# A delta rule's last norm traced in one piece, fewer filling steps around it and in the second attention, and another form of a recurrence's sigmoid

## Chip, cores and metric

One core of one Trainium2 chip runs the whole program in one launch. The metric is the device time of that launch in microseconds. The kernel before took 1979.86 us, the median of 3 runs (1976.52 to 1980.83).

## The reference, cut to what matters

The reference is two small transformer stacks in a row on a sequence of 256 positions and 1024 channels, all in float32. The first stack has two layers; each is a feed-forward block, a mixer, and a feed-forward block. The mixer sums three gated branches: a latent attention (mla), a gated delta rule (gdn) and a second attention (moba; with 256 positions and blocks of 256 it is plain causal attention). The second stack has an even and an odd layer; the odd mixer joins a gated linear recurrence with a dilated attention.

```python
# gated delta rule, chunks of 64 positions, one after the other
v_new = u_i - w_i @ state
o_i   = q_i @ state + qk_i @ v_new
state = state * exp(gl_i) + k_i.T @ v_new
...
o = rms_norm(o, out_norm) * silu(z)          # o over 128 values of one head

# linear recurrence of the odd mixer
r = sigmoid(xc @ w_a + b_a)
i = sigmoid(xc @ w_x + b_x)
log_a = -8.0 * r * softplus(-lam)
a  = exp(log_a)
bt = sqrt(-expm1(2.0 * log_a)) * (i * xc)
h_t = a_t * h_(t-1) + bt_t
```

## The kernel before, in words

**Matrix products.** Every large product is made in three passes: operand and weight are each split into a rounded high part and the remainder, a low part. `chunk` (L254) loads a chunk of weights into a staging tile `st` on SyncE's queue (3 buffers) and splits it in pieces of up to 1024 columns: ScalarE writes the high part `whi` (L281), VectorE the low part `wlo` (L282), with 3 buffers each. `mm3` (L287) issues the three matmuls of one contraction block (L290, L291, L292); the third reads the low part of the weights where weights are the stationary operand.

**Filling.** Small, latency-bound work (attention heads, the delta rule) is a Python generator that yields where it would wait; large projections are generators too, which yield after each 12 matmuls. `_mix` (L187) steps the first and pulls from the second at a fixed ratio per yield, `_weave` (L201) alternates. A pull that begins a projection also calls `chunk` for its weights, and the pull after its last step evacuates it.

**Order.** The scheduler of the framework orders each engine's instructions by program order and a simulated timeline; an instruction that is ready in the simulation may go ahead of an earlier one that is not. From the inversion to the scan of the delta rule, TensorE alone is under `manual_schedule`: it keeps the order of tracing exactly, while VectorE, ScalarE and GpSimd do not. `issue_after(ins)` adds an edge, so that what is traced in the block on the engine of `ins` is queued behind `ins`.

**The mixer** (L679 and following). The second attention is mixed with the generator `keys` (L718) at 2.05: what is left of the earlier filling, then the preparation of the delta rule's keys woven with the first merge and half of a gate projection. Its heads go in four pairs; `attend_o` makes six transposes of the scores (pPT), copies them to PT (L625, ScalarE) and multiplies them with the values (pOT). Then the generator `rest` (L741), 32 steps, fills `gdn_invert` (0.65, woven with `gdn_rest`), `gdn_solve` (1.65) and `gdn_scan` (1.5): half a gate projection (8 steps), a merge (8), and the two halves of the last gate projection (16, four per chunk of weights). The last merge, which follows, reads the scan's result in its high and low parts `brh` and `brl`.

**`gdn_scan`** goes through four chunks c = 0 to 3. In each, TensorE adds two products in `po` (L1261, L1282); between them VectorE makes `gvn` (L1264) and the generator yields; ScalarE copies `po` to `on` (L1284, written `gon` in the profile), and it yields again. `norm(t, on)` squares on ScalarE, then reduces, takes a reciprocal square root (`rsqrt`, L313: twelve operations on four columns) and multiplies (L1242) on VectorE. `finish(t, on)` makes four transposes (pon), multiplies with the gate and splits into `brh` and `brl`.

**`lru_core`** (L1641) makes the recurrence's coefficients in two passes of 512 columns: VectorE takes the pre-activation out of PSUM negated (L1665), bounds it (L1668), ScalarE takes the exponential (L1669), VectorE adds 1 (L1671) and takes the reciprocal (L1672); ScalarE makes `la` and `lm`, later a square root. It fills the odd mixer's projections; the dilated attention (`dil_attn`) that follows has scores `dpr`, transposes pdPT, and as filling the product with the recurrence's result `yh`, `yl`.

Of the kernel before, what the change touches and what calls it, by code (L numbers as in the profile page):

```python
# [1 line left out]

# [1 line left out]

# [5 lines left out]
F32 = mybir.dt.float32  # L10
F32R = mybir.dt.float32r
I32 = mybir.dt.int32
AF = mybir.ActivationFunctionType
# [207 lines left out]
class _Net:  # L221
    def __init__(self, ctx, tc, w, x, params, consts, lru, out, pat, cat, np_, nc_):
        self.tc, self.nc, self.w, self.x_in, self.out = tc, tc.nc, w, x, out
        self.params, self.consts, self.lru = params, consts, lru
        self.pat, self.cat, self.n_params, self.n_consts = pat, cat, np_, nc_
        P = lambda name, bufs, **kw: ctx.enter_context(tc.tile_pool(name=name, bufs=bufs, **kw))
        ps = bass.MemoryType.PSUM
        self.keep = P("keep", 1)
        self.wst = P("wst", 3)
        self.whl = P("whl", 3)  # L230
        self.nrm = P("nrm", 1)
        self.acc = P("acc", 4, space=ps)
        self.misc = P("misc", 4, space=ps)
        self.tiny = P("tiny", 4)
        self.early = {}
        self.P = self.keep.tile([128, self.n_params], F32, name="P")
        self.C = self.keep.tile([128, self.cat["dil0"]], F32, name="C")

# [15 lines left out]
    def chunk(self, name, i, between=None):  # L254


        nc = self.nc
        if (name, i) in self.early:
            return self.early.pop((name, i))
        chunks = [(kt, sum(b - a for a, b in cols)) for cols, (_, kt) in STREAMS[name]]  # L260
        sizes = [128 * kt * cols for kt, cols in chunks]
        layer, j = divmod(i, len(chunks))
        off = layer * sum(sizes) + sum(sizes[:j])
        kt, cols = chunks[j]
        n = kt * cols
        st = self.wst.tile([128, WMAX], F32, tag="st", name="st")
        src = lambda a, m: bass.AP(tensor=self.w[name].tensor, offset=off + a, ap=[[n, 128], [1, m]])
        if between is None:
            nc.sync.dma_start(out=st[:, :n], in_=src(0, n))
        pieces = []  # L270
        step = WPIECE // cols
        for k0 in range(0, kt, step):
            kk = min(step, kt - k0)
            m = kk * cols
            if between is not None:
                between(k0)
                nc.sync.dma_start(out=st[:, k0 * cols:k0 * cols + m], in_=src(k0 * cols, m))
            s = st[:, k0 * cols:k0 * cols + m]
            hi = self.whl.tile([128, WPIECE], F32R, tag="whi", name="whi")
            lo = self.whl.tile([128, WPIECE], F32R, tag="wlo", name="wlo")  # L280
            self.hi = nc.scalar.activation(hi[:, :m], s, AF.Copy).ins  # L281
            nc.vector.tensor_tensor(lo[:, :m], s, hi[:, :m].bitcast(F32), op=OP.subtract)  # L282
            v = lambda t: t[:, :m].rearrange("p (k c) -> p k c", k=kk)
            pieces.append((k0, kk, v(hi), v(lo)))
        return pieces
# [393 lines left out]
    def mixer(self, l, gain):  # L679
        pool = lambda ctx, name, bufs, **kw: ctx.enter_context(  # L680
            self.tc.tile_pool(name=name, bufs=bufs, reuse_waits="tile", **kw))
        with ExitStack() as ctx:
# [5 lines left out]
            with ExitStack() as c2:  # L688
# [37 lines left out]

                got["gate2"] = []
                f2 = keys()
                brs[2] = _mix(self.heads(big, at, *self.moba_heads(at, *z), sc, nsc), f2, 2.05)
                _all(f2)  # L730
            with ExitStack() as c2:
                gp = pool(c2, "mxg", 1)
# [488 lines left out]
    def gdn_scan(self, big, wk, scal, out, us, sz, vq):  # L1221
# [12 lines left out]
        def norm(t, on):  # L1234

            junk = W("gj")
            nc.scalar.activation(junk, on, AF.Square)
            ss = self.tiny.tile([128, 4], F32, tag="sso", name="sso")
            nc.vector.reduce_sum(ss, h4(junk), axis=AX)
            nc.vector.scalar_tensor_tensor(ss, ss, 1.0 / 128, vq[:, 4 * t:4 * t + 4], op0=OP.mult, op1=OP.add)  # L1240
            r = self.rsqrt(ss, 4, "ro")
            nc.vector.tensor_tensor(h4(on), h4(on), bch(r), op=OP.mult)  # L1242
            return on

        def finish(t, on):
            p4 = h4(self.transposes("pon", lambda h: on[:, h * 128:(h + 1) * 128]))
# [6 lines left out]
        for c in range(4):  # L1253
# [26 lines left out]
            for h in range(4):  # L1280
                cc = slice(h * 128, (h + 1) * 128)
                mm(po[orow, cc], qkT[t][wr, h * 64:h * 64 + 64], vn[wr, cc],  # L1282
                   start=(c == 0 and h == 0), stop=True, skip_group_check=True)
            nc.scalar.activation(on[orow, :], po[orow, :], AF.Copy)  # L1284
            yield
            if c == 1:
                ons = [norm(0, on)]
            if c == 2:
                yield
                finish(0, ons[0])  # L1290
        r = norm(1, on)
        for _ in range(4):
            yield
        finish(1, r)
        yield
        return oh, ol

    def gdn_z(self, l, big, wk):
# [342 lines left out]
    def lru_core(self, big, wk, xc, wa, wx, hs):  # L1641
# [4 lines left out]
        nl = big.tile([128, 4], F32, name="nl")  # L1646
        nc.vector.tensor_scalar(nl, self.par("lru_lam", 4), -1.0, None, op0=OP.mult)
        self.softplus(sp, nl, 4)
        nc.vector.tensor_scalar(sp, sp, -8.0, None, op0=OP.mult)
        nb = big.tile([128, 8], F32, name="nb")  # L1650
        nc.vector.tensor_scalar(nb[:, 0:4], self.par("lru_ba", 4), -1.0, None, op0=OP.mult)
        nc.vector.tensor_scalar(nb[:, 4:8], self.par("lru_bx", 4), 0.5, None, op0=OP.mult)
        a, bt, m2 = B("la"), B("lb"), B("lm")
        yield
        for c in range(2):
            pr, pi = self.ps("plr"), self.ps("pli")
            for b in range(2):
                m = 2 * c + b
                nc.tensor.matmul(pr[:, b * S:(b + 1) * S], wa[:, m, :], xc[:, m, :], start=True, stop=True)
                nc.tensor.matmul(pi[:, b * S:(b + 1) * S], wx[:, m, :], xc[:, m, :], start=True, stop=True)  # L1660
            v = slice(2 * c, 2 * c + 2)
            r = wk.tile([128, 2, S], F32, tag="lr", name="lr")
            for b in range(2):
                m = 2 * c + b
                nc.vector.tensor_scalar(r[:, b, :], pr[:, b * S:(b + 1) * S], -1.0, nb[:, m:m + 1], op0=OP.mult, op1=OP.add)  # L1665
                nc.scalar.activation(bt[:, m, :], pi[:, b * S:(b + 1) * S], AF.Tanh, scale=0.5, bias=nb[:, 4 + m:5 + m])
            yield
            nc.vector.tensor_scalar(r, r, 80.0, None, op0=OP.min)  # L1668
            nc.scalar.activation(r, r, AF.Exp)  # L1669
            yield  # L1670
            nc.vector.tensor_scalar(r, r, 1.0, None, op0=OP.add)  # L1671
            nc.vector.reciprocal(r, r)  # L1672
            for b in range(2):
                m = 2 * c + b
                nc.scalar.activation(a[:, m, :], r[:, b, :], AF.Exp, scale=sp[:, m:m + 1])
                nc.scalar.activation(m2[:, m, :], r[:, b, :], AF.Tanh, scale=sp[:, m:m + 1])
            yield
            sq = wk.tile([128, 2, S], F32, tag="lsq", name="lsq")
            nc.gpsimd.tensor_tensor(sq, a[:, v, :], a[:, v, :], op=OP.mult)
            nc.vector.tensor_scalar(sq, sq, 1.0, -1.0, op0=OP.add, op1=OP.mult)  # L1680
            nc.gpsimd.tensor_tensor(m2[:, v, :], m2[:, v, :], sq, op=OP.mult)
            nc.vector.scalar_tensor_tensor(bt[:, v, :], bt[:, v, :], 1.0, xc[:, v, :], op0=OP.add, op1=OP.mult)
            yield
# [73 lines left out]
```

## Time and profile before

| | |
|---|---|
| median of 3 runs | 1979.86 us (1976.52 to 1980.83) |
| the profiled execution's own time | 1975.25 us |
| its span from first to last instruction | 1973.4 us |
| TensorE busy | 98% |
| VectorE busy | 78% |
| ScalarE busy | 55% |
| GpSimd busy | 6% |
| mean granted TensorE clock | 0.997 |

PE is TensorE's matmuls, PEld its weight loads, DVE is VectorE, ACT ScalarE, POOL GpSimd, SP SyncE. Times in rows are microseconds from the start of the span unless marked as ns. Where a tile is named `out<-in`, the instruction reads `in` and writes `out`; `L282` is line 282 of the kernel before. In a timeline the bracket at a row's end is the idle time before it and what released it.

### The profile page before, as it was taken

Reading aid. Unit: us, or ns where it says so; the run is one execution under the profiler, and the core shown is the slowest. Engines: PE = TensorE matmul, PEld = TensorE weight load, DVE = VectorE, ACT = ScalarE, POOL = GpSimd, SP = SyncE. Lnnn points to the kernel's source line nnn. Section 1 sums busy time; section 2 is a strip of 40 time slices with the busy share of each in tenths; the row PEclk is TensorE's granted clock in tenths of the full one; section 3 lists DMA queues with packets and bytes.
Section 4 is the critical chain, followed back from the end, with each engine's and each line's share of the span. In section 5 each row is a group of like instructions: output and inputs, shape, how many; then the busy total and the mean of one; then the engine's idle time right before and its main releaser. Section 6 shows DMA issues by size and latency. Waiting matters only on the chain.

```text
span 1973.4 us, 35062 instructions
## 1 busy us (share of the span) xinstructions
PE 1937.5 (98%) x14060; PEld 1772.7 (90%) x14060; DVE 1530.1 (78%) x2797; ACT 1091.0 (55%) x1766; POOL 122.8 (6%) x154
## 2 busy tenths in 40 slices
PE   7999999999999999999999999999999999989999
PEld 7889989899988988899898998889999989979998
DVE  6876889757787677769996678766978876978875
ACT  5555666534555555556664455554656654666653
POOL 0000130210000000001211100000000000210000
PEclk9999999999999999999999999999999999989999
DMA  6555544324555555554432345555245556426554
GB/s 243 190 184 191 178 154 145 108 87 143 181 190 182 202 176 190 187 183 182 150 129 87 108 171 184 187 188 188 90 167 180 186 178 215 147 76 213 177 179 137
DMA packets 50691, 327.18 MB, mean 166 GB/s; under 512 B 6624, under 2 KB 8672, under 8 KB 18528
## 3 DMA queue, kind: packets, MB, share of 16 engines
q1 hardware_dynamic: 49296, 324.09, 46.7%
q8 instruction: 110, 1.80, 0.4%
q10 hardware_dynamic: 1232, 0.85, 0.2%
q14 instruction: 53, 0.43, 0.1%
HBM read 323.87 MB, written 1.05 MB: 165 GB/s over the span
## 4 chain that ended last, share of the span: by engine, by line
PE 94%; DVE 4%; issue 1%; ACT 1%; DMA 0%; SPq 0%; DVEq 0%; ACTq 0%
PE pu L416 11%; PE pr L416 9%; PE pg L416 7%; PE pu L418 6%; PE pr L418 5%; PE pg L418 4%; PE pg L292 3%; PE pg L291 3%; PE pg L290 3%; PE pr L291 3%; PE pr L290 3%; PE pr L292 3%; PE pga L290 3%; PE pga L291 2%; PE pga L292 2%; PE pb L291 1%
## 5 line engine op out<-in xcount | busy, mean ns | idle before, releaser
L281 ACT ACTIVATE whi<-st 128x1024 fp32r<-128x1024 f32 (+2 forms) x628 | 650.7, 1037 | 696.0 <-PE pr L416 121.9
L282 DVE TENSOR_TENSOR wlo<-st,whi 128x1024 fp32r<-128x1024 f32 (+2 forms) x628 | 760.2, 1211 | 311.7 <-ACT whi L281 306.3
L416 PE MATMUL pu<-xx,whi 128*128 128x512 f32 x960 | 336.8, 395 | 0.0
L416 PE MATMUL pr<-gx,whi 128*128 128x512 f32 x792 | 272.3, 395 | 0.0
L418 PE MATMUL pu<-xx,wlo 128*128 128x256 f32 x960 | 264.1, 279 | 0.0
L416 PE MATMUL pg<-xx,whi 128*128 128x512 f32 x640 | 223.6, 394 | 0.0
L416 PEld LDWEIGHTS pu<-xx,whi 128*128 128x128 f32 x960 | 178.8, 188 | 39.3
L418 PE MATMUL pr<-gx,wlo 128*128 128x256 f32 x792 | 211.0, 279 | 0.0
L418 PEld LDWEIGHTS pu<-xx,wlo 128*128 128x128 f32 x960 | 180.8, 188 | 1.6
L418 PE MATMUL pg<-xx,wlo 128*128 128x256 f32 x640 | 175.7, 278 | 0.0
L416 PEld LDWEIGHTS pr<-gx,whi 128*128 128x128 f32 x792 | 144.4, 188 | 29.6
L418 PEld LDWEIGHTS pr<-gx,wlo 128*128 128x128 f32 x792 | 149.2, 188 | 5.4
L416 PEld LDWEIGHTS pg<-xx,whi 128*128 128x128 f32 x640 | 119.2, 188 | 26.7
L290 PE MATMUL pg<-xx,whi 128*128 128x256 f32 x448 | 128.0, 286 | 9.6 <-ACT whi L281 9.6
L292 PE MATMUL pg<-xx,wlo 128*128 128x256 f32 x448 | 127.9, 285 | 0.5 <-DVE wlo L282 0.5
L291 PE MATMUL pg<-xx,whi 128*128 128x256 f32 x448 | 127.6, 285 | 0.0
L418 PEld LDWEIGHTS pg<-xx,wlo 128*128 128x128 f32 x640 | 120.2, 188 | 1.1
L290 PE MATMUL pga<-xx,whi 128*128 128x256 f32 x384 | 112.2, 292 | 0.0
L291 PE MATMUL pga<-xx,whi 128*128 128x256 f32 x384 | 108.7, 283 | 0.0
L292 PE MATMUL pga<-xx,wlo 128*128 128x256 f32 x384 | 108.7, 283 | 0.0
L290 PEld LDWEIGHTS pg<-xx,whi 128*128 128x128 f32 x448 | 86.6, 193 | 10.6 <-ACT whi L281 9.6
L292 PEld LDWEIGHTS pg<-xx,wlo 128*128 128x128 f32 x448 | 86.5, 193 | 1.0 <-DVE wlo L282 0.8
(565 smaller groups left out, 4451.0 us busy)
## 6 DMA issues: line engine op xcount, KB each, us to landing
st<-in_w_in_dram SPq DMA_DIRECT2D x52, 1024.0 KB, 4.8
st<-in_ffb_w_in_dram SPq DMA_DIRECT2D x44, 1024.0 KB, 4.7
st<-in_ffa_w_in_dram SPq DMA_DIRECT2D x43, 1024.0 KB, 4.8
st<-in_ffn_w_gate_dram SPq DMA_DIRECT2D x22, 1024.0 KB, 4.8
st<-in_ffn_w_up_dram SPq DMA_DIRECT2D x22, 1024.0 KB, 4.7
st<-in_ffa_w_out_dram SPq DMA_DIRECT2D x16, 896.0 KB, 4.5
st<-in_ffb_w_out_dram SPq DMA_DIRECT2D x16, 896.0 KB, 4.5
st<-in_ffn_w_down_dram SPq DMA_DIRECT2D x16, 896.0 KB, 4.6
```

The costliest lines, as they stand in the source:

```text
L281: self.hi = nc.scalar.activation(hi[:, :m], s, AF.Copy).ins
L282: nc.vector.tensor_tensor(lo[:, :m], s, hi[:, :m].bitcast(F32), op=OP.subtract)
L290: mm(out, a[0], b[0], start=start, stop=False, **kw)
L291: mm(out, a[0], b[1], start=False, stop=False, **kw)
L292: mm(out, a[1], b[0], start=False, stop=stop, **kw)
L416: mm(p, hi[:, k, c], x.rearrange("p e s -> p (e s)"), start=first == k0 + k, stop=False, skip_group_check=True)
L418: mm(p[:, S:], lo[:, k, c], x[:, 0, :], start=False, stop=last == k0 + k, skip_group_check=True)
```

## The change

In `gdn_scan` the norm of the second half is traced inside chunk c = 3, before its last yield, instead of after it; two bare yields instead of four stand between there and `finish`. The norm's last multiplication is kept in `self.hold`, and while it is set, `chunk` queues each `wlo` behind it on VectorE. The ratio of the second attention's mix goes from 2.05 to 1.7. In `lru_core` the sigmoid is written as exp(min(x, 0)) * (1 + tanh(|x| / 2)), which is twice the sigmoid, with the factor 8 before the softplus halved to 4.

```diff
-        self.early = {}
+        self.early, self.hold = {}, None
...
             self.hi = nc.scalar.activation(hi[:, :m], s, AF.Copy).ins
-            nc.vector.tensor_tensor(lo[:, :m], s, hi[:, :m].bitcast(F32), op=OP.subtract)
+            with self.tc.issue_after(self.hold) if self.hold else nullcontext():
+                nc.vector.tensor_tensor(lo[:, :m], s, hi[:, :m].bitcast(F32), op=OP.subtract)
...
-                brs[2] = _mix(self.heads(big, at, *self.moba_heads(at, *z), sc, nsc), f2, 2.05)
+                brs[2] = _mix(self.heads(big, at, *self.moba_heads(at, *z), sc, nsc), f2, 1.7)
...
             r = self.rsqrt(ss, 4, "ro")
-            nc.vector.tensor_tensor(h4(on), h4(on), bch(r), op=OP.mult)
-            return on
+            return on, nc.vector.tensor_tensor(h4(on), h4(on), bch(r), op=OP.mult).ins
...
             nc.scalar.activation(on[orow, :], po[orow, :], AF.Copy)
+            if c == 3:
+                last, self.hold = norm(1, on)
             yield
             if c == 1:
-                ons = [norm(0, on)]
+                first, _ = norm(0, on)
             if c == 2:
                 yield
-                finish(0, ons[0])
-        r = norm(1, on)
-        for _ in range(4):
-            yield
-        finish(1, r)
+                finish(0, first)
+        for _ in range(2):
+            yield
+        finish(1, last)
         yield
+        self.hold = None
         return oh, ol
...
-        nc.vector.tensor_scalar(sp, sp, -8.0, None, op0=OP.mult)
+        nc.vector.tensor_scalar(sp, sp, -4.0, None, op0=OP.mult)
         nb = big.tile([128, 8], F32, name="nb")
-        nc.vector.tensor_scalar(nb[:, 0:4], self.par("lru_ba", 4), -1.0, None, op0=OP.mult)
...
             r = wk.tile([128, 2, S], F32, tag="lr", name="lr")
+            ra = wk.tile([128, 2, S], F32, tag="lsq", name="lra")
             for b in range(2):
                 m = 2 * c + b
-                nc.vector.tensor_scalar(r[:, b, :], pr[:, b * S:(b + 1) * S], -1.0, nb[:, m:m + 1], op0=OP.mult, op1=OP.add)
+                x, ba = pr[:, b * S:(b + 1) * S], self.par("lru_ba", 1, m)
+                nc.scalar.activation(ra[:, b, :], x, AF.Abs, bias=ba)
+                nc.vector.tensor_scalar(r[:, b, :], x, ba, 0.0, op0=OP.add, op1=OP.min)
                 nc.scalar.activation(bt[:, m, :], pi[:, b * S:(b + 1) * S], AF.Tanh, scale=0.5, bias=nb[:, 4 + m:5 + m])
             yield
-            nc.vector.tensor_scalar(r, r, 80.0, None, op0=OP.min)
+            nc.scalar.activation(ra, ra, AF.Tanh, scale=0.5)
             nc.scalar.activation(r, r, AF.Exp)
             yield
-            nc.vector.tensor_scalar(r, r, 1.0, None, op0=OP.add)
-            nc.vector.reciprocal(r, r)
+            nc.vector.scalar_tensor_tensor(r, ra, 1.0, r, op0=OP.add, op1=OP.mult)
```

## Rows read from the trace of the kernel before

**Rows 1.** The page, busy us of each engine, share of the span and instructions.

```profile
PE 1937.5 (98%) x14060; PEld 1772.7 (90%) x14060; DVE 1530.1 (78%) x2797; ACT 1091.0 (55%) x1766; POOL 122.8 (6%) x154
```

**Rows 2.** PE's waits: what it waited for, us in total, times, longest us.

```profile
PE pdPT L1627 <- DVE dpr L1614: 3.9, 1, 3.9
PE pOT L299 <- ACT PT L625: 3.9, 4, 1.4
PE pb L290 <- ACT brh L307: 3.2, 2, 1.6
PE pr L291 <- DVE yl L308: 1.7, 1, 1.7
...
PE pb L291 <- DVE brl L308: 1.2, 2, 0.6
...
PE po L1282 <- DVE gvn L1264: 0.8, 2, 0.4
```

**Rows 3.** Windows: busy us (instructions) per engine, granted clock, DMA share, GB/s.

```profile
465.70:469.10 3.40, 3.20 (x15) 3.20 (x16) 0.14 (x1) 0.00 (x0) 0.00 (x0) 0.50 0.10 39
...
1745.70:1755.90 10.20, 5.51 (x24) 5.14 (x25) 8.47 (x28) 5.85 (x15) 0.00 (x0) 0.50 0.07 26
```

**Rows 4.** Windows of tile pb alone, PE, PEld, DVE, clock; layer 0, layer 1.

```profile
464.50:475.20 10.70, 10.04 (x70) 9.84 (x71) 1.35 (x2) 0.84 0.28 106
1138.20:1148.90 10.70, 10.03 (x82) 9.83 (x83) 1.36 (x2) 1.00 0.41 157
```

**Rows 5.** Window of tile pga alone, between the last po and pon, layer 0.

```profile
449.30:460.90 11.60, 11.59 (x96) 11.57 (x96) 1.38 (x2) 1.00 0.45 171
```

**Rows 6.** Timeline of VectorE, the scan of layer 0: start, duration, instruction.

```profile
434.55 0.68 DVE L1239 TENSOR_REDUCE sso<-gj 128x4 f32<-128x512 f32 x1
...
436.32 0.15 DVE L318 TENSOR_SCALAR rors<-sso 128x4 int32<-128x4 int32 x1
...
437.70 0.16 DVE L324 SCALAR_TENSOR_TENSOR rors<-rorst,rors 128x4 f32<-128x4 f32 x1
...
440.73 0.69 DVE L1242 TENSOR_TENSOR gon<-gon,rors 128x512 f32<-128x512 f32 x1
...
443.29 1.23 DVE L282 TENSOR_TENSOR wlo<-st,whi 128x1024 fp32r<-128x1024 f32 x1 [0.28 <-ACT whi L281]
...
446.31 1.22 DVE L282 TENSOR_TENSOR wlo<-st,whi 128x1024 fp32r<-128x1024 f32 x1
...
465.16 0.68 DVE L308 TENSOR_TENSOR brl<-gj,brh 128x512 fp32r<-128x512 f32 x1
```

**Rows 7.** Timeline of ScalarE, norm(1) of layer 0.

```profile
450.05 0.63 ACT L1237 ACTIVATE gj<-gon 128x512 f32<-128x512 f32 x1
```

**Rows 8.** Timeline of PE, the second attention's end in layer 0.

```profile
372.80 0.43 PE L299 MATMUL pOT<-PT,mv 128*64 128x256 f32 x1 [1.13 <-ACT PT L625]
...
375.17 0.43 PE L299 MATMUL pOT<-PT,mv 128*64 128x256 f32 x1 [0.69 <-ACT PT L625]
```

**Rows 9.** Timeline of ScalarE, the same stretch.

```profile
371.31 1.06 ACT L281 ACTIVATE whi<-st 128x1024 fp32r<-128x1024 f32 x1 [0.81 <-PE pga L291]
```

**Rows 10.** Lines, VectorE, 1687 to 1753 us: busy us, mean ns, idle before.

```profile
L1672 DVE RECIPROCAL lr<-lr 128x512 f32<-128x512 f32 x2 | 6.7, 3348 | 0.0
...
L1682 DVE SCALAR_TENSOR_TENSOR lb<-lb,xc 128x512 f32<-128x512 f32 x2 | 1.4, 682 | 0.0
...
L1668 DVE TENSOR_SCALAR lr<-lr 128x512 f32<-128x512 f32 x2 | 0.8, 416 | 0.0
```

**Rows 11.** Window, all engines: PE, PEld, DVE, ACT, POOL, clock.

```profile
1720.00:1753.00 33.00, 27.21 (x165) 22.01 (x164) 32.93 (x68) 22.14 (x37) 8.61 (x5) 0.89 0.19 65
```

**Rows 12.** Lines, ScalarE, 1687 to 1753 us.

```profile
L1610 ACT ACTIVATE dpr<-dpr,dmx 128x384 f32<-128x384 f32 (+1 forms) x4 | 3.1, 766 | 1.5 <-DVE dmx L1608 1.5
...
L1666 ACT ACTIVATE lb<-pli,nb 128x256 f32<-128x256 f32 x4 | 1.7, 468 | 0.3 <-PE pli L1660 0.3
...
L1684 ACT ACT_TABLE_LOAD x1 | 1.3, 1283 | 0.0
```

More of the change, by code (lines that the diff above doesn't have):

```diff
@@ L1 @@
-from contextlib import ExitStack
+from contextlib import ExitStack, nullcontext
 import numpy as np
```

## The prediction

> **What bounds the kernel now.** I read the page's busy times first: TensorE (PE) is busy 1937.5 of 1973.4 us [rows 1], so only about 36 us of its idle time can be won, and work on another engine counts only where PE waits for it. The view of PE's waits says where [rows 2]. The waits this change can reach are one in the odd mixer's second attention (pdPT, 3.9 us, for VectorE's normalised scores), one there on the low part yl (1.7), four in the first block's attentions (pOT, 3.9 together), and at the delta rule's end pb on brh and on brl (3.2 and 1.2 over the two layers) and po on gvn (0.8). A change of 0.2%, 4.0 us, is about what a measurement can tell from none.
>
> A wait can cost more than itself. While PE worked through the stretch after layer 0's pb waits the granted clock was 0.50, half of 2.4 GHz, and again from 1745.7 to 1755.9 us after the pdPT wait [rows 3]. In equal stretches of 10.7 us from the pb wait, 70 matmuls started in layer 0 (mean clock 0.84) and 82 in layer 1 (1.00) [rows 4]: 12 matmuls, about 1.4 us at the 0.12 us of a full-speed one (11.59 us for 96 [rows 5]).
>
> **Part one, the scan's end.** PE's order here is the order of tracing. The filling generator has 32 steps of 12 matmuls, 1.45 us each [rows 5]. Thirteen go before the scan (10 in the inversion, where 9 of 19 turns go to the side work, and 3 in the solve); the scan's 13 yields at 1.5 take the other 19: after yields 7, 8, ... 13 the running total is 10, 12, 13, 15, 16, 18, 19. So steps 24 to 31 stand between the last po and the transposes pon, which are the 96 matmuls of [rows 5], and step 32 alone between pon and merge.
>
> Now the new order. norm(1) is traced ahead of the eighth yield, so ahead of steps 24 and 25. Two yields follow instead of four before finish: pon comes after step 28, and steps 29 to 32 stand between it and merge.
>
> *Gain.* In the old order brl ends at 465.84 [rows 6], 4.9 us after pon (460.93, behind the 96 matmuls), weights' splits in between included; four steps are 5.8 us. So pb's waits go: 1.6 + 0.6 per layer. po's 0.4 goes too, because the weights' low part that ran on VectorE at 446.31 [rows 6], ahead of gvn, is now queued elsewhere. That is 2.6 per layer.
>
> *Cost.* A filling step is also where the next chunk of weights is split. Step 25 opens the second gate projection (steps 25 to 28), and its chunk is traced when self.hold is already set. Its two low parts ran at 443.29 and 446.31 [rows 6], long before; now both must follow the norm's last multiplication. The wait is added in front of PE: step 25's third matmul reads that low part, and behind it in PE's queue stand the rest of the filling, pon and merge, that is, everything. When does the low part arrive? The square of gon starts at 450.05 and is done at 450.68 [rows 7]. Then VectorE: the reduction 0.7, thirteen four-column operations 2.3 (nine of them start from 436.32 to 437.70 in norm(0), 0.17 apart), the multiplication 0.7, the low part 1.2 [rows 6]: 450.7 + 4.9 = 455.6. PE wants it at 451.0, after step 24 (1.45) and two matmuls from 449.3 on. **A new wait of 4.6 us per layer** at least; 5.3 if the gate's evacuation (0.7), which step 25 also traces, slips in. I take 4.9, between them. What is late next is covered: the second low part comes 1.2 later and PE needs it 2.7 later. The loads keep their order on SP's queue, and nothing on POOL stands between.
>
> *Clock.* Both layers' new waits are longer than the 2.2 us after which layer 0 fell and layer 1 did not. I take a fall in both, 1.4 each, where 1.4 was paid already: +1.4. The bounds are no fall (-1.4) and 2.75 each, the odd mixer's loss below (+4.1).
>
> The Trainium skill, page "TensorE: Matmul & The Clock Gate", section "What's actually happening", says that the slow clock is the default and that activity releases it; that is a rule against any change that leaves PE idle longer in one piece. By it the fall comes in both layers, as taken; layer 1's 2.2 us without a fall shows that not every wait brings it.
>
> Sum of part one: 2 x (4.9 - 2.6) + 1.4 = **+6.0 us** (+2.6 to +9.5).
>
> **Part two, the second attention's ratio, 2.05 to 1.7.** The filler has 39 steps (17 left over, 8 merge, 8 gate, 6 of keys). At 2.05 they are used up at main yield 20 of 27, at 1.7 at yield 23. So the third head pair's pOT gets steps ahead of it and the last pair's still has none. In layer 0 they wait 1.13 and 0.69 [rows 8]; with 0.69 again, 1.4 is left of the 3.9 for layer 1's third pair. But the 1.13 came from a weights' high part, 1.06 us at 371.31 [rows 9], that ran between the pair's two copies PT, and it ran there because the last filling had just freed its buffer. When the filling's end moves to the last pair, so does that 1.06: 1.1 + 1.4 less 2 x 1.06 leaves **-0.4 us**. Ends: -3.9 (all waits go) and +0.8 (the gate's tanh, 0.62, slips in as well). Weight loads move by at most 11 steps with their chunks on SP's queue; PE's list shows no wait for a load [rows 2], so I cost them at nothing, hidden under earlier chunks.
>
> **Part three, the recurrence's sigmoid.** Per pass, VectorE loses a reciprocal of 3.35 us, a min (0.42) and an add of the same form and gains a scalar_tensor_tensor of 128x512 (0.68, as L1682) [rows 10]; the evacuation keeps its form. That is 3.5 us less, 7.0 in two passes, where VectorE is busy 32.93 of 33 us [rows 11]. The small negated bias goes as well (under 0.2). ScalarE gains two Abs (0.47 each, the price of L1666 from the same kind of source [rows 12]) and a Tanh (under 2 x 0.47): 1.9 per pass, and it is busy 22.14 of those 33. The second pass's reciprocal stands on VectorE's queue ahead of the scores whose normalisation PE waits for; the exponentials waited 1.5 us for VectorE's maxima and not for a table [rows 12]. With 3.5 us less there and an earlier square root, the scores should be ready about when PE arrives. So 3.9 and 1.7 go, and with them the half clock: PE was busy 5.51 us in that stretch [rows 3], half of it, 2.75, lost. **-8.4 us**; bounds -8.4 and 0 (the third rival).
>
> No row shows Abs. Around the square root a table load of 1.28 us appears [rows 12]; Copy, Square, Tanh and Exp run between without. If Abs needed one at each change to Tanh, up to eight would be 10.3 us of ScalarE; I take none, as for those four.
>
> The Trainium skill, page "ScalarE: Activation LUTs", section "Table sets: the hidden batching unit", puts abs into every set; by it there is none.
>
> **Sum**: 6.0 - 0.4 - 8.4 = -2.8 us. The profiled execution took 1975.25 (span 1973.4), 4.6 below the median 1979.86; I apply the difference to the median: **1977.1 us**.
>
> **Rivals.**
> 1. *The clock does not fall after the new waits*, as in layer 1 before. Then part one is 4.6 - 1.4 = 3.2 and the total -5.6: 1974.3. For it: that layer; against: the new wait is over twice as long, in one piece.
> 2. *The held low parts are not step 25's*, if that chunk is traced before the hold. Then there is no new wait and part one gains 5.2 and layer 0's 1.4: total -15.4, 1964.5. For it: only that the count of steps could be one out; against: the 96 matmuls fit the count.
> 3. *Slower*: in the odd mixer the exponentials wait for ScalarE instead, which takes the Abs and Tanh ahead of the square root's two table loads; 1.9 us more there outweighs the 1.5 us that VectorE cost them, pdPT waits as before and the clock falls again. Part three is then 0 and the total +5.6: 1985.5. It decides once part three keeps less than 5.6 (slower than before), less than 1.6 (by over 0.2%). Against it: ScalarE idles 11 of 33 us and the reciprocal's chain to the square root shortens.
>
> **Chances.** Forecast 0.62, rivals 0.15, 0.08, 0.15. The forecast's own range, from its bounds without the furthest, is 1972 to 1984. The range of 1970 to 1986 leaves out rival 2 and part of rival 3. Faster by over 4.0 us: rival 2, two thirds of rival 1, and about three tenths of the forecast, 0.37. Slower: two thirds of rival 3 and a little of the forecast, 0.13. Within 0.2%: 0.50.
>
> **What would show it.** PE's waits: a new one of about 5 us in each layer, on a low part in a gate projection (pga); none on brh or brl; pdPT's and yl's gone. VectorE's order: no low part between reduction and multiplication of norm(1), two right behind it. Clock rows of 0.50 after the new waits, none at the odd mixer. The forecast is wrong if no such pga wait stands there (rival 2), or if pdPT still waits over 2 us (rival 3).

## The result, and the profile after

The changed kernel takes **1990.12 us** (median of 6 runs, 1988.23 to 1996.54) where the kernel before takes 1977.33 in the runs beside it (6 runs, 1976.04 to 1980.83): a ratio of 1.0073, 95% interval 1.0061 to 1.0085. That is 12.8 us slower. The forecast was 1977.1, 2.8 us below the 1979.86 that it started from, and its range ended at 1986. The profiled execution took 1988.39 (span 1986.6 against 1973.4, mean granted clock 0.992 against 0.997). The line numbers are one to five higher than before.

PE's waits of the kernel after, in the columns of [rows 2]:

```profile
PE pga L293 <- DVE wlo L283: 10.8, 2, 5.4
...
PE pT L1156 <- DVE gM L1175: 4.5, 2, 2.5
PE pdL L300 <- DVE dmx L1605: 3.1, 1, 3.1
PE pr L291 <- ACT yh L311: 1.6, 1, 1.6
PE pOT L300 <- ACT PT L626: 1.4, 2, 0.7
...
PE pr L292 <- DVE yl L312: 0.7, 1, 0.7
```

Against [rows 2]: pdPT, yl on L308, brh, brl and gvn are gone, and pOT has fallen from 3.9 to 1.4. In their place stand three waits that were not there (pdL had one of 0.2): pga for a low part, as forecast; pT for gM in the inversion, and pdL in the odd mixer, which were not forecast. Their places, from PE's timeline after (start, duration, instruction, and in brackets the idle time before it and its releaser):

```profile
379.26 0.37 PE L1156 MATMUL pT<-gM,gF 64*64 64x64 f32 x2 [2.53 <-DVE gM L1175]
...
459.19 0.58 PE L293 MATMUL pga<-xx,wlo 128*128 128x256 f32 x1 [5.38 <-DVE wlo L283]
...
1058.93 0.27 PE L1156 MATMUL pT<-gM,gF 64*64 64x64 f32 x2 [2.00 <-DVE gM L1175]
...
1137.45 0.58 PE L293 MATMUL pga<-xx,wlo 128*128 128x256 f32 x1 [5.38 <-DVE wlo L283]
```

The clock is the other half. These are all stretches of the kernel after, up to its tail, in which the granted clock was 0.50, 1.2 GHz of 2.4, called half clock from here on (windows view, columns as in [rows 3]):

```profile
379.10:382.50 3.40, 3.24 (x38) 3.15 (x39) 0.68 (x3) 0.77 (x2) 2.04 (x3) 0.50 0.02 5
457.60:464.40 6.80, 5.21 (x24) 5.21 (x25) 3.80 (x4) 0.33 (x1) 0.00 (x0) 0.50 0.44 154
1136.80:1143.60 6.80, 6.15 (x29) 6.15 (x30) 3.04 (x4) 1.06 (x1) 0.00 (x0) 0.50 0.42 154
1457.70:1461.10 3.40, 3.40 (x18) 3.40 (x17) 0.96 (x6) 0.50 (x1) 0.00 (x0) 0.50 0.01 4
1471.40:1474.80 3.40, 3.40 (x17) 3.40 (x18) 0.41 (x1) 0.00 (x0) 0.14 (x2) 0.51 1.00 405
1751.20:1758.00 6.80, 5.65 (x25) 4.41 (x25) 6.80 (x22) 3.22 (x5) 0.00 (x0) 0.50 0.10 36
```

Before there were two, 3.4 and 10.2 us long [rows 3]. The loss in such a stretch is half of PE's busy time in it, since an idle PE loses nothing: 13.5 us of loss after (27.05 busy), 4.4 before (3.20 and 5.51 busy). Each trace is one execution, and the stretches differ between executions (see the end).

Where the 13.2 us of span came in, from the starts of the same matmul in the two traces (before, after):

| up to | before | after | gained (-) or lost here |
|---|---|---|---|
| layer 0's inversion (pF) | 375.97 | 374.97 | -1.0 |
| end of that inversion (pvq) | 409.57 | 412.59 | +4.0 |
| behind layer 0's scan and last merge (pst) | 512.61 | 518.97 | +3.3 |
| layer 1's inversion (pF) | 1049.68 | 1055.16 | -0.9 |
| end of that inversion (pvq) | 1083.28 | 1090.85 | +2.1 |
| behind layer 1's scan and last merge (pst) | 1184.92 | 1197.66 | +5.2 |
| behind the even mixer (pst) | 1480.42 | 1495.95 | +2.8 |
| behind the odd mixer (pst) | 1792.74 | 1805.82 | -2.5 |

The scan lost 8.5, the inversion after the second attention 6.1, the even mixer, whose code did not change, 2.8 (its two half-clock stretches, 6.8 us fully busy, are worth 3.4 of loss), and the odd mixer gave back 2.5 where 8.4 was forecast.

Three stretches of VectorE's timeline show the three new waits being made. First the norm of layer 0's last half:

```profile
453.61 0.69 DVE L775 TENSOR_TENSOR gate<-pga,R 128x512 f32<-128x512 f32 x1 [2.65 <-PE pga L293]
454.22 0.68 DVE L1240 TENSOR_REDUCE sso<-gj 128x4 f32<-128x512 f32 x1
...
457.31 0.69 DVE L1243 TENSOR_TENSOR gon<-gon,rors 128x512 f32<-128x512 f32 x1
457.92 2.35 DVE L283 TENSOR_TENSOR wlo<-st,whi 128x1024 fp32r<-128x1024 f32 x2
```

The gate's eviction did slip in ahead of the reduction, and the two low parts follow the norm's product at once; PE takes the first at 459.19. Second, the start of the inversion, after:

```profile
374.38 0.68 DVE L775 TENSOR_TENSOR gate<-pga,R 128x512 f32<-128x512 f32 x1
374.98 1.21 DVE L283 TENSOR_TENSOR wlo<-st,whi 128x1024 fp32r<-128x1024 f32 x1
376.11 2.34 DVE L1120 TENSOR_TENSOR kbe<-kr,gf 128x512 f32<-128x512 f32 x2
378.38 0.41 DVE L309 TENSOR_TENSOR brl<-pOT,brh 128x256 fp32r<-128x256 f32 x1
378.71 0.73 DVE L1175 TENSOR_TENSOR gM<-eye,pF 128x256 f32<-128x256 f32 x2
```

and before:

```profile
371.38 0.69 DVE L774 TENSOR_TENSOR gate<-pga,R 128x512 f32<-128x512 f32 x1
372.40 1.23 DVE L282 TENSOR_TENSOR wlo<-st,whi 128x1024 fp32r<-128x1024 f32 x1 [0.33 <-ACT whi L281]
...
374.47 1.28 DVE L1119 TENSOR_TENSOR kbe<-kr,gf 128x512 f32<-128x512 f32 x2
...
376.85 0.74 DVE L1174 TENSOR_TENSOR gM<-eye,pF 128x256 f32<-128x256 f32 x2
```

With the ratio 1.7 the filling lasts to the attention's end, and its last gate eviction comes 3.0 us later. Behind it stand the low part, two kbe products, brl and only then gM, for which PE waits. Before, kbe was done at 375.75, when pF had not begun (375.97).

Third, the odd mixer, where PE waits at pdL until 1752.35. After, the four scans run ahead of the first score reduction (VectorE's timeline, first of each kind):

```profile
1745.98 3.52 DVE L1693 TENSOR_TENSOR_SCAN lh<-la,lb 128x256 f32<-128x256 f32 x4
...
1751.74 0.55 DVE L1605 CUSTOM_DVE_ANT_0 dpr<-pdL,dil 128x384 f32<-128x384 f32 x1
```

Before, they came behind all six reductions of the first heads and two of the next:

```profile
1735.82 0.55 DVE L1602 CUSTOM_DVE_ANT_0 dpr<-pdL,dil 128x384 f32<-128x384 f32 x1
...
1743.92 2.43 DVE L1688 TENSOR_TENSOR_SCAN lh<-la,lb 128x256 f32<-128x256 f32 x4
```

### The profile page after: what moved, and what is told of

Same layout as the page of the kernel before. It is cut to its first block, busy times and chain, and to the rows that moved or that the text cites. A ratio compares the mean times of both kernels' runs of the same rounds, so it can differ in the third digit from the quotient of the medians.

```text
span 1986.6 us, 35051 instructions
## 1 busy us (share of the span) xinstructions
PE 1945.7 (98%) x14060; PEld 1780.6 (90%) x14060; DVE 1531.1 (77%) x2792; ACT 1091.3 (55%) x1772; POOL 127.6 (6%) x154
## 4 chain that ended last, share of the span: by engine, by line
PE 93%; DVE 5%; issue 1%; ACT 1%; DMA 0%; SPq 0%; DVEq 0%; ACTq 0%
PE pu L417 11%; PE pr L417 9%; PE pg L417 7%; PE pu L419 6%; PE pr L419 5%; PE pg L419 4%; PE pr L291 3%; PE pr L292 3%; PE pr L293 3%; PE pg L293 3%; PE pg L291 3%; PE pg L292 3%; PE pga L291 3%; PE pga L293 2%; PE pga L292 2%; DVE wlo L283 2%
## 5 line engine op out<-in xcount | busy, mean ns | idle before, releaser
L283 DVE TENSOR_TENSOR wlo<-st,whi 128x1024 fp32r<-128x1024 f32 (+2 forms) x628 | 762.6, 1216 | 314.3 <-ACT whi L281 308.8
L293 PE MATMUL pg<-xx,wlo 128*128 128x256 f32 x448 | 127.6, 285 | 0.5 <-DVE wlo L283 0.5
L293 PE MATMUL pga<-xx,wlo 128*128 128x256 f32 x384 | 111.7, 291 | 10.8 <-DVE wlo L283 10.8
L291 PE MATMUL pga<-xx,whi 128*128 128x256 f32 x384 | 114.7, 299 | 0.0
L292 PE MATMUL pga<-xx,whi 128*128 128x256 f32 x384 | 111.5, 290 | 0.0
L293 PEld LDWEIGHTS pg<-xx,wlo 128*128 128x128 f32 x448 | 86.3, 193 | 1.0 <-DVE wlo L283 0.8
```

The costliest lines, as they stand in the source:

```text
L291: mm(out, a[0], b[0], start=start, stop=False, **kw)
L292: mm(out, a[0], b[1], start=False, stop=False, **kw)
L293: mm(out, a[1], b[0], start=False, stop=stop, **kw)
```

## The experiments

All ratios are to the kernel before, run on the same chip beside each. The experiments ran on several chips, so a difference between the medians of two of them is less sure than one between their ratios.

### Each part alone

`scan_only`: the diff's hunks in `chunk` and `gdn_scan`, with the hold; ratio 2.05 and the old `lru_core`.

```diff
+            if c == 3:
+                last, self.hold = norm(1, on)
             yield
...
-        for _ in range(4):
+        for _ in range(2):
             yield
```

> The kernel before with the scan's part alone (norm(1) before the eighth yield, the hold, two bare yields). Theory, the hold makes PE wait: a wait of 5.4 us on a weights' low part in a gate projection (pga) in each layer, with the clock at 0.50 behind it, no wait on brh or brl, 6 to 10 us slower than before. Rival, the wait comes only with the other two parts' shifts: no pga wait over 1 us, 4 to 7 us faster.

Measured: 1985.81 us, ratio 1.0033 (1.0022 to 1.0043), so 6.5 us slower. The pga wait is the same (waits view: `PE pga L293 <- DVE wlo L283: 10.7, 2, 5.4`), with 6.8 us of half clock in each layer, and nothing waits on brh or brl. That is what the theory expected.

`ratio_only`:

```diff
-                brs[2] = _mix(self.heads(big, at, *self.moba_heads(at, *z), sc, nsc), f2, 2.05)
+                brs[2] = _mix(self.heads(big, at, *self.moba_heads(at, *z), sc, nsc), f2, 1.7)
```

> The kernel before with the ratio 1.7 alone. Theory, the later filling pushes VectorE's work past the attention's end: the pOT wait shrinks by about 0.5 us net and a new wait of 2.0 to 2.5 us on gM stands at the inversion's first product (pT) in each layer, 2 to 6 us slower. Rival, my forecast: no new wait, 0 to 1 us faster.

Measured: 1987.03, ratio 1.0030 (1.0017 to 1.0044). The ratio alone, costed at -0.4, loses about 6 us, the upper end of its theory; its waits view has the pT wait of the whole change:

```profile
PE pT L1155 <- DVE gM L1174: 4.2, 2, 2.5
...
PE pOT L299 <- ACT PT L625: 1.7, 2, 1.0
```

`lru_only`: the diff's hunks in `lru_core`.

```diff
+                nc.scalar.activation(ra[:, b, :], x, AF.Abs, bias=ba)
+                nc.vector.tensor_scalar(r[:, b, :], x, ba, 0.0, op0=OP.add, op1=OP.min)
...
-            nc.vector.reciprocal(r, r)
+            nc.vector.scalar_tensor_tensor(r, ra, 1.0, r, op0=OP.add, op1=OP.mult)
```

> The kernel before with the recurrence's sigmoid alone. Theory, the freed time of VectorE goes to the recurrence's later steps, which now stand ahead of the scores: pdPT's wait goes and one of about 3 us on pdL takes its place, with the clock at 0.50 there, 1 to 4 us faster. Rival, my forecast: no wait over 1 us in that stretch and no half clock, 7 to 9 us faster.

Measured: 1977.86, ratio 0.9996 (0.9986 to 1.0005): no change that can be told, where the theory expected 1 to 4 us. Its waits are right: those at pdPT and yl are gone, and `PE pdL L299 <- DVE dmx L1602: 3.1, 1, 3.1` is new. The windows view has the half clock:

```profile
1740.00:1750.20 10.20, 10.20 (x39) 7.45 (x38) 8.00 (x26) 5.30 (x11) 0.00 (x0) 0.50 0.15 52
```

As long a stretch at half clock as before, 10.2 us, but PE is busy in all of it, where before it was busy 5.51 and idle in its waits for the rest [rows 3].

The three parts add up to 1.0059, about 11.7 us of the 14.4 that the ratio 1.0073 makes of 1977; the gap lies within the parts' intervals, each some 2 us to either side.

### The scan: which part of it loses

`scan_nohold`: as `scan_only`, without the hold.

```diff
-                last, self.hold = norm(1, on)
+                last, _ = norm(1, on)
```

> The scan's part alone without the hold (norm(1) early, two bare yields, low parts free). Theory: no pga wait and none on brh or brl, 3 to 7 us faster than before. Rival: low parts cut into the norm as before, the transposes pon wait up to 4 us for it instead, within 2 us of before.

Measured: 1983.25, ratio 1.0015 (1.0004 to 1.0026). The pga wait goes, but pon waits 3.18 in each layer, as the rival said, at 3.0 us slower by the ratio, 1 us more than it allowed. VectorE's timeline shows why: low parts and an eviction stand between the four-column operations of the norm.

```profile
453.01 0.68 DVE L1240 TENSOR_REDUCE sso<-gj 128x4 f32<-128x512 f32 x1
453.61 1.22 DVE L283 TENSOR_TENSOR wlo<-st,whi 128x1024 fp32r<-128x1024 f32 x1
...
456.25 1.23 DVE L283 TENSOR_TENSOR wlo<-st,whi 128x1024 fp32r<-128x1024 f32 x1 [0.36 <-ACT whi L281]
...
459.13 1.23 DVE L283 TENSOR_TENSOR wlo<-st,whi 128x1024 fp32r<-128x1024 f32 x1
460.28 0.15 DVE L325 SCALAR_TENSOR_TENSOR rors<-rorst,rors 128x4 f32<-128x4 f32 x1
460.47 0.69 DVE L1243 TENSOR_TENSOR gon<-gon,rors 128x512 f32<-128x512 f32 x1
```

So a hold is needed: with only two filling steps, these low parts make pon late. The question is which low parts to hold.

`scan_latehold`: the hold is set one yield (two filling steps) later, behind filling step 25, so that its chunk is free and only the last chunk (steps 29 to 32) is held.

```diff
-                last, self.hold = norm(1, on)
+                last, held = norm(1, on)
...
+        self.hold = held
         for _ in range(2):
             yield
```

> The scan part alone, but the hold is set two turns later, so that step 25's low parts are made as in the kernel before and only later ones queue behind the norm's product. Theory (the loss of the scan part is TensorE's wait for step 25's held low part, 5.4 us, and the half clock behind it, per layer): the pga wait is gone in both layers, the waits at the norm's transposes and at brh and brl stay gone or fall below 1 us, and the run is 6 to 9 us shorter than the scan part alone (1985.8), that is 1976 to 1980, at or 1 to 2 us below the kernel before (1978). Rival (the loss is the two fewer filling steps, whatever is held): pon waits of 3 us a layer as without a hold, 1982 to 1984.

Measured: **1970.18, ratio 0.9959 (0.9945 to 0.9972)**. It beats both kernels: 7.5 us below the median of the kernel before beside it, 20 below the changed kernel, and 15.6 below `scan_only` (14.6 by the ratios). That is 6 us below the range of the theory; theory and rival differed in the waits, and there the theory holds: in the windows shown, from the scan's end over pon into the filling, PE is never idle, at full clock, in both layers (windows view), and no wait on brh or brl is left:

```profile
450.00:465.00 15.00, 15.00 (x126) 14.83 (x126) 11.43 (x26) 7.77 (x10) 0.00 (x0) 1.00 0.42 145
1126.00:1140.00 14.00, 14.00 (x120) 14.00 (x119) 10.96 (x14) 6.28 (x8) 0.15 (x2) 1.00 0.42 151
```

In VectorE's order the norm's product starts at 456.26, where without a hold it was 460.47, with the last chunk's low parts right behind:

```profile
456.26 0.69 DVE L1243 TENSOR_TENSOR gon<-gon,rors 128x512 f32<-128x512 f32 x1
456.87 2.35 DVE L283 TENSOR_TENSOR wlo<-st,whi 128x1024 fp32r<-128x1024 f32 x2
```

They are done at 459.2, and PE does not wait for them.

`scan_4y`: the norm early, no hold, four steps ahead of the transposes as before.

```diff
-        for _ in range(2):
+        for _ in range(4):
             yield
```

> The last norm early, no hold, and all four filling steps before its transposes left in place. Theory (the pon waits of 3.2 us a layer without a hold come from two filling steps too few ahead of the transposes): the pon waits go, and the run is 1976 to 1980, 3 to 6 us shorter than with two steps (1983.3). Rival (VectorE is so full there that the norm ends late in any case): pon waits above 2 us a layer remain and the run stays at 1982 to 1984.

Measured: 1979.88, ratio 1.0005 (0.9995 to 1.0016). The pon waits go, as the theory says, but brh and brl wait 1.6 and 0.6 in each layer again, as before. So the early norm alone is worth nothing; the two steps moved behind pon are what covers brh and brl, and the late hold is what lets them move.

### The ratio: why the inversion waits

`ratio_prio` asked the scheduler for a higher priority for gM, but the order stayed as in `ratio_only` on every engine; it is a second measurement of the same instructions and does not tell theory and rival apart.

```diff
+            with self.tc.high_priority():
+                nc.vector.tensor_tensor(h4(M[t]), bcm(ident), h4(p[:, :256]), op=OP.subtract)
```

> The ratio 1.7 alone, and the inversion's first VectorE product (gM) ahead of other VectorE work. Theory (the ratio's cost is that gM comes 2.0 to 2.5 us late behind the gate's eviction, a low part and kbe): the pT waits fall below 0.5 us in both layers, and the run is 1978 to 1983, 4 to 8 us shorter than the ratio alone (1987.0). Rival (the cost is the later start of the whole inversion, less covered at its end, and the clock): the pT waits go, or half of them, and the run stays within 2 us of 1987.

Measured: 1986.89, ratio 1.0041 (1.0027 to 1.0055).

`ratio_kbe` puts kbe behind gM with an edge that the scheduler must keep:

```diff
-            nc.vector.tensor_tensor(h4(kbe[t]), h4(kr[t]), bch(f[:, t, 1, :]), op=OP.mult)
...
+            with self.tc.issue_after(self.first_m):
+                nc.vector.tensor_tensor(h4(kbe[t]), h4(kr[t]), bch(f[:, t, 1, :]), op=OP.mult)
```

> The ratio 1.7 alone, and the two kbe products (2.3 us beside GpSimd) queued on VectorE behind the inversion's first gM products. Theory (they are what stands ahead of gM and makes the 2.5 and 1.7 to 2.0 us waits at pT): the pT waits fall below 0.5 us and the run is 1979 to 1984, 3 to 8 us shorter than the ratio alone (1987.0); the pOT waits stay shorter than in the kernel before, 0.7 and 1.0 in place of 1.8 and 2.1. Rival (gM is late for another reason, the later start of the inversion or GpSimd's gF): pT waits above 1.2 us remain and the run stays within 2 us of 1987.

Measured: 1978.84, ratio 1.0005 (0.9995 to 1.0014), about 8 us less than `ratio_only` by the medians and 5 by the ratios. PE's waits have no pT any more, and pOT stays at 1.7. VectorE's timeline:

```profile
377.77 1.21 DVE L282 TENSOR_TENSOR wlo<-st,whi 128x1024 fp32r<-128x1024 f32 x1
378.91 0.41 DVE L308 TENSOR_TENSOR brl<-pOT,brh 128x256 fp32r<-128x256 f32 x1
379.24 0.73 DVE L1175 TENSOR_TENSOR gM<-eye,pF 128x256 f32<-128x256 f32 x2
379.90 2.05 DVE L1135 TENSOR_TENSOR kbe<-kr,gf 128x512 f32<-128x512 f32 x2
```

So kbe ahead of gM made that wait. With it out of the way the ratio itself is worth nothing that can be measured; why the 2.2 us saved at pOT (3.9 to 1.7) do not show in the time stays open.

### The gate part: where its 8.4 us went

`lru_prio`: the same request for the dilated attention's score reductions; again the order stayed that of `lru_only`, on every engine.

```diff
+                with self.tc.high_priority():
                     for e in range(2):
```

> The gate part alone, and the dilated attention's first score reductions ahead of other VectorE work in program order. Theory (the time freed on VectorE went to the two scans, the step up and low parts, which stand ahead of the first score reduction, so TensorE waits 3.1 us at pdL for a buffer, with half clock behind it): the pdL wait falls below 1 us, less half clock in the odd mixer, and the run is 1971 to 1976, 2 to 6 us shorter than the gate part alone (1977.9). Rival (the scans then end later and the next steps wait for them instead): waits at yl or pdPT of 2 us and more come back, 1977 to 1980.

Measured: 1977.18, ratio 0.9992 (0.9982 to 1.0002): `lru_only` once more.

`lru_late` traces the scans and what follows them between the first steps of the attention, with an edge from the score reductions to the scans; only the edge is shown:

```diff
+                    if i in (1, 2):
+                        c = i - 1
+                        with self.tc.issue_after(self.scored):
+                            scans[0](c)
```

> The gate part alone, and the two pairs of scans queued on VectorE behind the second score reduction, so that the first four reductions come about 3.6 us earlier (four scans at 0.73 and a product at 0.66). Theory (the freed VectorE time went to the scans, which stand ahead of the scores, and that makes the 3.1 us wait at pdL): the pdL wait falls below 0.5 us, half clock in the odd mixer shrinks, and the run is 1971 to 1976, 2 to 7 us shorter than the gate part alone (1977.9). Rival (VectorE is full either way, and the next step behind it is late instead): a wait of 2 us and more at pdPT or at yl comes back, 1977 to 1981.

Measured: 1978.80, ratio 0.9997 (0.9986 to 1.0007). The pdL wait falls from 3.09 to 0.97, so VectorE's order did make it, and no wait of 2 us takes its place. But the time does not move, since half clock lasts longer, with PE busy all through:

```profile
1739.50:1756.60 17.10, 17.10 (x62) 12.74 (x61) 14.05 (x41) 7.56 (x14) 0.00 (x0) 0.50 0.12 32
```

Neither theory had that.

`lru_fill`: three filling steps to two of the dilated attention's.

```diff
-            _mix(self.dil_attn(wk, dil, qT, kT, v, yh, yl, (q, k), values), fill, 1.0)
+            _mix(self.dil_attn(wk, dil, qT, kT, v, yh, yl, (q, k), values), fill, 1.5)
```

> The gate part alone, and three filling steps to two of the dilated attention in place of one to one. Theory (TensorE comes to the scores too early for VectorE; more projection work between them covers the pdL wait, and what follows at half clock is shorter): pdL wait below 1 us, 1973 to 1977. Rival (the filling work runs out and waits at pr for yl or at pdPT for the scaled scores come instead, with the same half clock): waits of 2 us and more there, 1977 to 1982.

Measured: 1977.62, ratio 0.9997 (0.9984 to 1.0009). The pdL wait is still 3.09, and neither pdPT nor yl waits: both are wrong. Half clock lasted 13.7 us.

### The parts together again

`after_latehold`: the changed kernel with the hold set later, as in `scan_latehold`.

> The changed kernel whole, with the hold set two turns later so that step 25's low parts are free. Theory (the held low part of step 25 is the largest loss of the change, and the parts add up): as the late hold was worth 15.6 us to the scan part alone (1985.8 to 1970.2), 1974 to 1980 in place of 1990.1; what is left above the scan part alone (1970.2) is the ratio's 5 to 9 us. Rival (the ratio moves the work so that the held wait comes at another chunk): a low-part wait of 3 us and more is seen at pga or pb, and the run is 1982 to 1990.

Measured: 1982.91, ratio 1.0013 (1.0002 to 1.0023), 3 us above the expected range, without the rival's wait; 7.2 us less than the changed kernel by the medians, 12 by the ratios. No pga or pb wait is left. The pT waits (2.52 and 1.72) and 20.5 us of half clock in the odd mixer are left.

`after_mended`: that and kbe behind gM, as in `ratio_kbe`.

> The changed kernel whole with both repairs: the hold set two turns later, and the kbe products behind the first gM products. Theory (the held low part of step 25 and kbe ahead of gM are together the loss of the change, and the parts add up): no pga wait, no pT wait, no brh, brl and pon waits, only the 3.1 us wait at pdL; 1968 to 1974, the late-hold scan's 1970.2 with a ratio and a gate part that are each worth nothing within 2 us. Rival (the losses overlap, or half clock in other layers eats the gain): 1975 to 1983, with the waits gone all the same.

Measured: 1977.37, ratio 0.9987 (0.9976 to 0.9998). The waits are gone as expected, the time is the rival's:

```profile
1734.70:1755.20 20.50, 20.43 (x76) 15.65 (x77) 13.49 (x44) 8.12 (x16) 0.00 (x0) 0.50 0.18 51
```

`scan_ratio` and `lru_scan_latehold` each leave one part of that out (the gate part; the ratio and kbe).

> The late-hold scan part with the ratio 1.7 and kbe behind gM, without the gate part. Theory (the gate part is what keeps the mended change at 1977 rather than 1970, through half clock in the odd mixer: 20.5 us there against 10.2 in the late-hold scan part alone): 1968 to 1973, and half clock of about 10 us in the odd mixer. Rival (the ratio is what costs it): 1975 to 1979 with 10 us of half clock in the odd mixer, more of it elsewhere.

Measured: 1974.53, ratio 0.9978 (0.9968 to 0.9988).

> The late-hold scan part with the gate part, ratio 2.05 as before. Theory (same as above: the gate part costs what it wins, and more where half clock lasts longer): 1972 to 1977, a pdL wait of 3.1 us and 10 to 20 us of half clock in the odd mixer. Rival (the gate part is worth nothing here too): 1968 to 1972.

Measured: 1971.16, ratio 0.9970 (0.9959 to 0.9980), with the pdL wait of 3.09 and

```profile
1732.90:1739.70 6.80, 5.84 (x26) 4.52 (x26) 6.80 (x21) 3.03 (x5) 0.00 (x0) 0.50 0.13 27
```

Adding the gate part to the late-hold scan is worth nothing (1971.2 to 1970.2; its rival). Adding the mended ratio costs some 4 us (1974.5; the intervals just touch), between theory and rival, with 10.2 us of half clock in the odd mixer and 10.2 in the even one. Neither alone explains 1977 for all three; half clock does. Each run's time multiplied by its mean granted clock is an estimate of the time at full clock (too low where PE idles at half clock): on average 1963.7 for `scan_latehold`, 1964.4 for `lru_scan_latehold`, 1963.8 for `scan_ratio` and 1963.3 for `after_mended`, and 1969.2 to 1969.8 for the kernel before in the same sets of runs. So, by this estimate, with neither the pga nor the pT wait the scan's gain is there in all four, and what sets them apart is the clock.

## Why the prediction was wrong

**Part one, +6.0 forecast, +6.5 measured alone: the mechanism right, the clock's term too small.** The wait stands where step 25 was counted to be, 5.38 us against 4.9, and brh, brl and gvn wait no more. The 5.3 named there for a gate eviction slipping in is what happened. The clock fell in both layers. In the rows after, layer 0 pays 5.38 less the 2.6 saved, and a clock loss of 2.6 (5.21 busy, halved) less 1.6 before, +3.8 (start differences show +3.3); layer 1 pays 5.38 - 2.6 + 3.1 = +5.9 (+5.2). The clock was put at 1.4 a layer and took 2.6 and 3.1, so that +6.5 lies so near to +6.0 is in part luck. Rivals 1 (no fall) and 2 (another chunk held) did not happen here. `scan_latehold` is rival 2 made on purpose: it was priced 12.6 us below the forecast (-15.4 against -2.8), and measured 15.6 below `scan_only` (14.6 by the ratios).

**Part two, -0.4 forecast, about +6 measured: the first step that failed.** The forecast costed the four pOT waits and what could slip between ScalarE's copies, and asked nothing of VectorE. pOT's waits did fall, from 3.9 to 1.4, by more than was costed. But the filling that now lasts to the attention's end leaves its eviction, low part and kbe on VectorE at the moment when the inversion begins, and the first product there, gM, is one that PE must have: 2.53 and 2.00 us, and in this execution half clock behind the first. What is late next was asked of one engine only. `ratio_kbe` shows both halves: without kbe ahead of gM the waits go, and the ratio is worth nothing.

**Part three, -8.4 forecast, -0.8 (-2.8 to +1.0) measured: the step that weighed most.** The operations cost what was said: 0.686 for the new product, 0.476 for an Abs, 0.62 for a Tanh, and no table load beside the Abs. By the Trainium skill, page "ScalarE: Activation LUTs", section "Table sets: the hidden batching unit", there is none, and the trace agrees. The two waits went. The step that failed is "and with them the half clock". It rested on reading the half clock as something that the pdPT wait brings; but [rows 3] has it from 1745.7, and that wait, 3.94 us long, ends at 1748.69, so the clock had fallen 0.95 us into it. The odd mixer's loss is its waits and half of what PE does at half clock:

| kernel | waits, us | busy at half clock, us | waits + half | less 8.4 | by start differences |
|---|---|---|---|---|---|
| before | 3.94 + 1.70 | 5.51 | 8.4 | | |
| `lru_only` | 3.09 | 10.20 | 8.2 | -0.2 | +0.1 |
| after | 3.13 | 5.65 | 6.0 | -2.4 | -2.5 |
| `lru_scan_latehold` | 3.09 | 5.84 | 6.0 | -2.4 | -2.5 |
| `lru_late` | 0.97 + 0.75 | 17.10 | 10.3 | +1.9 | +2.3 |
| `after_mended` | 3.11 | 20.43 | 13.3 | +4.9 | +4.0 |

The sum follows the measured difference within 1 us in each row. So the waits saved are real, and the clock took them back: before, nearly half of the slow stretch fell on time in which PE waited anyway; in `lru_only` all of it falls on work. And a wait took the place of the two: with 7 us less of VectorE's work ahead of them, the scans went ahead of the scores, and PE met the late reductions at pdL, 3.1 us. `lru_late` shows the order to be its cause (0.97 with the scans behind).

Rival 3 had the value right for this part (0, total 1985.5) and the mechanism wrong: PE waits at pdL for VectorE, not for ScalarE. The even mixer's +2.8, from half clock in code that did not change, no case held. It is not shown to come from the change: `lru_prio` lost as much there in the order of the kernel before.

**The chances.** The 0.13 for slower was two thirds of rival 3 and a little of the forecast. No case had a wait made by the ratio, and clock loss was allowed for only behind the scan's waits.

By the Trainium skill, page "TensorE: Matmul & The Clock Gate", section "What's actually happening", slow is the default and activity releases it. The trace agrees after the two waits of 5.38; the rule does not tell `lru_late`, where PE waits 0.97 and is then busy, from kernels with 3.1.

What stays open: what sets the moment at which the clock falls in the odd mixer, and with it whether half clock lasts 6.8 us or 20.5 behind the same 3.1 us wait (the table at the end). More filling beside the scores was tried once (`lru_fill`) and changed neither the wait nor the time.

## What to carry to other kernels

When weights' splits are queued behind a chain, count which chunk the next filling step opens: holding one chunk too early cost some 15 us here, and the same edit one yield later is the best version measured, 1970.18 (with the gate part, 1971.16, it cannot be told apart). When a filling is stretched to the end of a stage, list what it leaves on every engine at the next stage's first product, not only on the engine whose waits it shortens. A wait that is followed by half clock is worth its length only if the half clock goes with it, and that has to be looked at in the new trace: half of PE's busy time in such stretches belongs in the sum. One trace does not say where a kernel loses to the clock: the same order of instructions can have such a stretch in one execution and none in the next.

## What the runs showed that was not expected

- Half clock does not follow the waits one to one, nor the code. `lru_only` and `lru_prio` have the same order of instructions on every engine and the same waits of 1.6 and 0.6 on brh and brl. Behind them the clock stays full in the one (first row, `lru_only`) and falls in the other (`lru_prio`):

```profile
468.40:471.80 3.40, 3.40 (x29) 3.40 (x30) 0.00 (x0) 0.63 (x1) 0.00 (x0) 1.00 0.06 24
...
468.40:471.70 3.30, 3.30 (x18) 3.30 (x17) 0.00 (x0) 0.00 (x0) 0.00 (x0) 0.50 0.02 5
```

  `lru_prio` also has half clock behind layer 1 and in two stretches of the even mixer, `lru_only` in neither. In the same way `ratio_only` and `ratio_prio` have one order of instructions, and the clock fell behind the first pT wait in the one only.
- In the odd mixer six traced kernels have the same order of instructions on every engine, and in each PE waits 3.1 us at pdL until 68.3 us after the mixer's start. What differs is when the clock fell, and in these six traces the length goes with it (us from the matmul pst ahead of the mixer, from the traces):

| kernel | clock fell at | half clock lasted |
|---|---|---|
| after | 67.2 | 6.8 |
| `lru_scan_latehold` | 67.3 | 6.8 |
| `after_latehold` | 68.0 | 20.5 |
| `after_mended` | 68.2 | 20.5 |
| `lru_only` | 70.3 | 10.2 |
| `lru_prio` | 70.3 | 10.2 |

- The clock moves the time by itself: the same kernel `scan_ratio` gave 1968.21 us at a mean granted clock of 0.997 and 1976.02 at 0.994.
- Some VectorE operations were slower beside GpSimd. Each kbe product took 0.68 us before. After, the first two took 2.34 together, while GpSimd's gN and gF ran from 375.20 on (GpSimd's timeline, after):

```profile
375.20 1.57 POOL L1174 TENSOR_TENSOR gN<-eye,gF 128x256 f32<-128x256 f32 x1 [2.36 <-PE pOT L303]
376.74 1.17 POOL L1165 TENSOR_TENSOR gF<-A,C 128x256 f32<-128x256 f32 x1
```

  GpSimd pays as well: its gN took 0.73 before, from 376.20, where kbe was already done. The low part that VectorE had begun at 374.98, ahead of gN, took its usual 1.21: in these rows the operation that began while the other engine's ran was the slower one. Part of the first pT wait is this: an estimate of 1.1 us, 2.34 less the 1.28 that the two took before.
